# S5 outer products in a pool of their own, temporaries shared with the powers, a third read-back buffer

## The chip, the core and the metric

One core of a Trainium2 chip runs the whole program in one launch. TensorE does the matrix products and transposes, VectorE and ScalarE the elementwise work and the evacuation of PSUM, GpSimd a few powers, and SyncE issues the DMAs. The metric is the time of one execution on the device in microseconds, as the median of several runs.

## The reference

Two layers of a trunk with three branches (gated linear attention, latent attention, an S5 state space model) run over 512 latent tokens and 128 prompt tokens, with the same weights. The change touches only the S5 branch:

```
bu = einsum('blgp,gnp->blgn', u.reshape(b, n, 32, 16), b_re + i b_im)
for d in (forward, backward):
    ab, cf = discretise(a[d], log_dt[d])         # per group and state
    x = scan(x[t] = ab * x[t-1] + cf * bu[t])    # complex, over the tokens
    y += Re(einsum('blgn,gpn->blgp', x, c))
out = glu(gelu(y + d_skip * u)); new_state_s5 = last x of each direction
```

`new_state_s5` and the S5 output of both token groups are results or feed them.

## The kernel before, in words

All tokens stand side by side (640 columns). Weights are streamed through SBUF in halves of 128x512: SyncE loads a raw tile `wraw`, ScalarE casts it to `whi`, VectorE subtracts to get the residue `wlo`, and TensorE multiplies three times (high by high, high by residue, residue by high). Each of these tiles has four buffers. `h` is the normalised input, made of a cast on ScalarE and a residue on VectorE too, once per layer and 128 rows.

The S5 branch works in chunks of 8 tokens, 80 chunks in all. Its input projection is written to DRAM (`sud`) and read back with one chunk to a partition: `s5_in` does that in four blocks, each with a read-back (`s5cr`, SyncE), a cast into another order (`s5cg`, ScalarE), eight transposes (line 824, TensorE) and a copy to `U`. Ahead of it, `s5_kernel` makes the kernel within a chunk; its tiles (`s5ks` among them) are written to DRAM by four `kd` DMAs. After it, `s5_z` turns chunk inputs into chunk states in 16 steps n, one for each block b of four groups and each direction d. A step's front forms `s5r` by three VectorE operations over 128x512 (a first product, line 736; a second product into `s5rtmp`, line 737; an add, line 738), transposes it on TensorE (line 845) and copies it to `s5pm` on ScalarE. Its back, one step later, multiplies `s5pm` with `U`. `s5_pow` forms the first 16 powers of the chunk's transition by four doublings of six VectorE operations (lines 890 to 895); the scan behind `s5_z` needs them.

TensorE's order is written out by hand: `fill(n)` puts n steps of a waiting projection between the S5 steps, each step six products of 320 columns (line 247). On the other engines a scheduler sets the order from priorities and its own estimate of time. The S5 stage has a raised priority, the powers a lowered one within it (`POW`). Pools are stacked: a pool that is opened after another has closed takes its memory, and a tile in it waits for the readers and writers of the tiles that lay there. `s5i` and `s5z` thus lie in the same place one after the other, and `s5i` lies where the tiles of `s5_kernel` lay.

Of the kernel before, what the change touches and what calls it, by code (L numbers as in the profile page):

```python
# [10 lines left out]
F32 = mybir.dt.float32  # L11
# [12 lines left out]
NC8 = 80  # L24
NB = 16
# [161 lines left out]
POW = 300  # L187
# [16 lines left out]
class Prog:  # L204
# [16 lines left out]
    def pool(self, name, bufs=1, **kw):  # L221
        return self.es.enter_context(self.tc.tile_pool(name=name, bufs=bufs, **kw))
# [586 lines left out]
    def s5_in(self, pa, p, fill):  # L809

        sud = self.sud[self.l]
        U = pa.tile([128, 32, NC8], F32, name="s5u")
        for cb in range(4):
            cr = p.tile([NC8, 8, 128], F32, name="s5cr", tag="s5cr", bufs=2)
            c = slice(128 * cb, 128 * cb + 128)
            self.S.dma_start(cr, sud[:, c].rearrange("(c j) x -> c j x", j=8))
            cg = p.tile([NC8, 8, 8, 16], F32, name="s5cg", tag="s5cg", bufs=1)
            self.copy(cg, cr.rearrange("c j (g x) -> c g j x", g=8))
            fill(FILL[0] if cb == 0 else FILL[1])
            for hf in range(2):  # L820
                ps = self.bank()
                for i in range(4):
                    g = 4 * hf + i
                    self.T.transpose(ps[:, NC8 * i:NC8 * i + NC8], cg[:, g].rearrange("c j x -> c (j x)"), self.ident[0:NC8, 0:NC8])
                g0 = 8 * cb + 4 * hf
                self.copy(U[:, g0:g0 + 4, :], ps[:, 0:4 * NC8].rearrange("p (g c) -> p g c", g=4))
        self.U = U

    def s5_z(self, p, fill):
        V = self.V  # L830

        X = self.mx().rearrange("p (c g) -> p c g", g=32)
        XZ = (X[:, 0:81], X[:, 82:162])
        sh = [128, 4, 8, 16]
        def front(b, d):
            r = p.tile([128, 4, 8, 16], F32, name="s5r", tag=f"s5r{d}", bufs=2 + d)
            tmp = p.tile([128, 4, 8, 16], F32, name="s5rtmp", tag=f"s5rtmp{d}", bufs=1)
            g = slice(32 * d + 4 * b, 32 * d + 4 * b + 4)
            w = [self.w[:, :, i, g].rearrange("p e g -> p g e") for i in range(2)]
            if d == 0:  # L840
                w = [x[:, :, ::-1] for x in w]
            self.outer(V, p, r, tmp, w[0], w[1], self.B1[:, 4 * b:4 * b + 4], self.B2[:, 4 * b:4 * b + 4], sh)
            ps = self.bank()
            for i in range(4):
                self.T.transpose(ps[:, 128 * i:128 * i + 128], r[:, i].rearrange("p a b -> p (a b)"), self.ident)
            pm = p.tile([128, 512], F32, name="s5pm", tag="s5pm", bufs=3)
            self.copy(pm, ps)
            return pm

        def back(b, d, pm):  # L850
            pz = self.bank()
            for i in range(4):
                self.mm(pz[:, NC8 * i:NC8 * i + NC8], pm[:, 128 * i:128 * i + 128], self.U[:, 4 * b + i, :])
            z = pz[:, 0:4 * NC8].rearrange("p (g c) -> p c g", g=4)
            gs = slice(4 * b, 4 * b + 4)
            if d == 0:
                self.copy(XZ[0][:, 1:81, gs], z)
            else:
                self.copy(XZ[1][:, 0:79, gs], z[:, 1:80])

        todo = []
        for n in range(16):
            todo.append((n // 2, n % 2, front(n // 2, n % 2)))
            if n:
                back(*todo.pop(0))
            fill(FILL[2])
        back(*todo.pop(0))
        x0 = self.vec("x0")
        V.tensor_copy(X[:, 81, :], XZ[1][:, 63, :])
        V.tensor_copy(XZ[0][:, 0, :], x0[:, 0:32])  # L870
        V.tensor_copy(XZ[1][:, 63, :], x0[:, 32:64])
        V.memset(XZ[0][:, 64, :], 0.0)
        V.memset(XZ[1][:, 79, :], 0.0)
        self.X, self.XZ = X, XZ

    def s5_pow(self, p):

        pt = p.tile([128, 2, NB, 64], F32, name="s5pt")
        V = self.V
        for i in range(2):  # L880
            V.tensor_copy(pt[:, i, 0], self.ab[:, i])
        n = 1
        while n < NB:
            sh = [128, n, 64]
            a, b = (pt[:, i, 0:n] for i in range(2))
            c, d = (pt[:, i, n - 1][:, None, :].to_broadcast(sh) for i in range(2))
            t1 = p.tile([128, NB // 2, 64], F32, name="sp1", tag="sp1")[:, 0:n]
            t2 = p.tile([128, NB // 2, 64], F32, name="sp2", tag="sp2")[:, 0:n]
            o = [pt[:, i, n:2 * n] for i in range(2)]
            V.tensor_tensor(t1, a, c, op=ALU.mult)  # L890
            V.tensor_tensor(t2, b, d, op=ALU.mult)
            V.tensor_tensor(o[0], t1, t2, op=ALU.subtract)
            V.tensor_tensor(t1, a, d, op=ALU.mult)
            V.tensor_tensor(t2, b, c, op=ALU.mult)
            V.tensor_tensor(o[1], t1, t2, op=ALU.add)
            n *= 2
            yield
        self.pt = pt
# [588 lines left out]
    def fill(self, n):  # L1487

        for _ in range(n):
            while self.stand:  # L1490
                try:
                    next(self.stand[0])
                    break
                except StopIteration:
                    self.stand.pop(0)
# [24 lines left out]
    def layer(self, l, x):  # L1520
        tc = self.tc
        self.l = l
        self.layer_vecs()
        pool = lambda n, **kw: self.pool_(n, l, **kw)
        run = lambda g: [None for _ in g]
        step = lambda g, n: [next(g, None) for _ in range(n)]
        fill = self.fill
# [5 lines left out]
        if l == 0:  # L1533
# [8 lines left out]
            g = pair(0, 8000)  # L1542
            both(g, 2)
            n = self.h_rstd()
# [5 lines left out]
        else:  # L1550
            g = self.h_rstd()
# [9 lines left out]
        es, ek, pk, pa, pz, kern = self.s5  # L1561
# [25 lines left out]
        pk.close()  # L1587
        self.late_vecs()
        with tc.high_priority(2000):
            with pool("s5i") as p:  # L1590
                self.s5_in(pa, p, fill)
            ep = ExitStack()
            pt = ep.enter_context(pool("s5t", side="right"))
            with tc.high_priority(-POW):
                for _ in self.s5_pow(pt):
                    pass
            with pool("s5z") as p:
                self.s5_z(p, fill)
        ek.close()
        with ExitStack() as eg:  # L1600
            with es:
# [81 lines left out]
```

## Time and profile before

| | |
|---|---|
| median of 3 runs | 1574.49 us (1572.39 to 1583.06) |
| the profiled execution | 1574.24 us, span 1572.5 us |
| TensorE busy | 1506.5 us, 96% of the span |
| VectorE busy | 1054.3 us, 67% |
| ScalarE busy | 629.5 us, 40% |
| mean granted TensorE clock | 0.986 of 2.4 GHz |

TensorE is the engine that sets the time. Times in the rows are microseconds from the span's start; PE is TensorE, DVE VectorE, ACT ScalarE, SP SyncE. Layer 0 has its S5 stage at about 100 to 170, layer 1 at about 860 to 930.

### The profile page before, as it was taken

What the parts mean: (1) busy time and instruction counts of PE and PEld (TensorE: products, weight loads), DVE (VectorE), ACT (ScalarE), POOL (GpSimd) and SP (SyncE); (2) the same over time, 40 slices, a digit from 0 to 9 for tenths busy, and PEclk for the clock granted to TensorE, in tenths of its full rate; (3) what the DMA queues carried; (4) which work ended last, traced back from release to release, by engine and by line L of the source; (5) the groups of instructions that cost most, each with busy time, mean ns of one, the idle gap of its engine ahead of it and who ended that gap; (6) DMA issues with size and microseconds to landing.
All of it is one profiled execution on the core that took longest, in us unless ns stands there. A gap on an engine that the chain in (4) does not pass through costs nothing. (4 is left out here: it accounts for less than half of the span.)

```text
span 1572.5 us, 28798 instructions
## 1 busy us (share of the span) xinstructions
PE 1506.5 (96%) x11334; PEld 1436.7 (91%) x11334; DVE 1054.3 (67%) x2435; ACT 629.5 (40%) x1171; POOL 46.5 (3%) x48
## 2 busy tenths in 40 slices
PE   5998999999999999999999899999999999999998
PEld 3788999988999888898998899999999999888998
DVE  8979694796556536879577579645766563487662
ACT  3324323555444454322324442254544442633321
POOL 0000000011000000000000000001300000000000
PEclk9998999999999999999999999999999999999999
DMA  9451435243312221237753333442331223212253
GB/s 347 158 151 49 122 113 167 90 133 102 103 63 75 85 75 56 78 110 241 258 195 99 97 79 113 138 133 87 115 114 61 74 81 111 69 55 68 91 169 104
DMA packets 109656, 182.09 MB, mean 116 GB/s; under 512 B 12752, under 2 KB 31120, under 8 KB 109520
## 3 DMA queue, kind: packets, MB, share of 16 engines
q1 hardware_dynamic: 109520, 180.25, 36.3%
q8 instruction: 89, 1.46, 0.4%
q14 instruction: 47, 0.39, 0.1%
HBM read 150.41 MB, written 29.79 MB: 115 GB/s over the span
## 5 line engine op out<-in xcount | busy, mean ns | idle before, releaser
L247 PE MATMUL pj<-h,whi 128*128 128x320 f32 x3456 | 664.8, 314 | 0.2 <-DVE og L488 0.2
L247 PEld LDWEIGHTS pj<-h,whi 128*128 128x128 f32 x3456 | 541.7, 189 | 6.5 <-issue 5.1
L229 ACT ACTIVATE whi<-wraw 128x512 fp32r<-128x512 f32 x326 | 204.9, 630 | 517.3 <-PE pj L247 384.1
L247 PE MATMUL pj<-h,wlo 128*128 128x320 f32 x1728 | 397.6, 310 | 0.0
L238 DVE TENSOR_TENSOR wlo<-wraw,whi 128x512 fp32r<-128x512 f32 x326 | 223.9, 688 | 216.5 <-ACT whi L229 209.8
L247 PEld LDWEIGHTS pj<-h,wlo 128*128 128x128 f32 x1728 | 290.8, 189 | 0.0
L247 PE MATMUL pj<-og,whi 128*128 128x320 f32 x736 | 142.9, 314 | 2.4 <-DVE og L238 2.4
L247 PEld LDWEIGHTS pj<-og,whi 128*128 128x128 f32 x736 | 115.4, 189 | 6.9 <-DVE og L238 3.2
L247 PE MATMUL pj<-whi,h 128*128 128x512 f32 x256 | 86.6, 400 | 5.1 <-ACT h L232 4.4
L247 PE MATMUL pj<-og,wlo 128*128 128x320 f32 x384 | 87.8, 310 | 0.0
L247 PEld LDWEIGHTS pj<-whi,h 128*128 128x128 f32 x256 | 48.8, 192 | 17.4 <-ACT h L232 5.0
L247 PEld LDWEIGHTS pj<-og,wlo 128*128 128x128 f32 x384 | 64.5, 188 | 0.0
L232 ACT ACTIVATE P<-bank,smx 128x384 f32<-128x384 f32 x64 | 36.5, 576 | 49.8 <-DVE smx L1235 49.8
L238 DVE TENSOR_TENSOR Ptl<-bank,Pth 128x512 fp32r<-128x512 f32 x48 | 31.7, 687 | 31.1 <-ACT Pth L229 30.9
L232 ACT ACTIVATE th<-pj 128x640 f32<-128x640 f32 x72 | 49.7, 690 | 6.3 <-PE pj L247 6.2
L247 PE MATMUL pj<-wlo,h 128*128 128x512 f32 x128 | 50.6, 396 | 0.0
L247 PE MATMUL pj<-s5g,whi 128*128 128x320 f32 x256 | 48.1, 310 | 0.0
L247 PE MATMUL bank<-s5qy,mx 128*80 128x128 f32 x256 | 46.1, 302 | 0.0
L577 DVE SCALAR_TENSOR_TENSOR mx<-pj,ada,tmp 128x320 f32<-128x320 f32 (+2 forms) x48 | 18.1, 433 | 39.6 <-PE pj L247 37.5
L1231 DVE TENSOR_REDUCE smx<-bank 128x1 f32<-128x384 f32 (+1 forms) x72 | 36.5, 524 | 10.6 <-PE bank L247 10.0
L229 ACT ACTIVATE Pth<-bank 128x512 fp32r<-128x512 f32 x48 | 27.1, 596 | 35.3 <-PE bank L1256 35.3
L1421 DVE SCALAR_TENSOR_TENSOR st<-st,bl,bank 64x128 f32<-64x128 f32 x112 | 38.8, 347 | 3.5
(349 smaller groups left out, 2320.2 us busy)
## 6 DMA issues: line engine op xcount, KB each, us to landing
wraw<-wpk SPq DMA_DIRECT2D x358, 256.0 KB, 2.8
og<-wpk SPq DMA_DIRECT2D x48, 256.0 KB, 5.4
qd<-s5qk SPq DMA_DIRECT2D x32, 256.0 KB, 2.9
s5qy<-qd SPq DMA_DIRECT2D x32, 256.0 KB, 4.0
gd<-gt SPq DMA_DIRECT2D x16, 320.0 KB, 2.8
gt<-gd SPq DMA_DIRECT2D x16, 320.0 KB, 3.1
md<-th SPq DMA_DIRECT2D x16, 320.0 KB, 2.3
th<-md SPq DMA_DIRECT2D x16, 320.0 KB, 3.5
```

What stands on the lines that cost most here:

```text
L229: self.A.activation(out, in_, AF.Copy, scale=scale)
L232: self.A.activation(out, in_, f, **kw)
L238: (eng or self.V).tensor_tensor(lo, src, hi.bitcast(F32), op=ALU.subtract)
L247: self.T.matmul(out, lhsT, rhs, start=start, stop=stop, skip_group_check=True, **kw)
L577: V.scalar_tensor_tensor(xn[:, j, lo:hi], ps[:, i, lo - 320 * i:hi - 320 * i], self.ads[l, 2][r][:, j:j + 1], xr[:, lo:hi], op0=ALU.mult, ...
L1231: V.tensor_reduce(mx[:, i:i + 1], ps[:, 0:w], axis=AX.X, op=ALU.max)
L1421: V.scalar_tensor_tensor(out, st[r, c, :], bl[r, c:c + 1], pu[c][r], op0=ALU.mult, op1=ALU.add)
```

## The change

`s5r` and `s5rtmp` move from the pool `s5z` to a new pool `s5r`, which is opened ahead of `s5i`, so that it lies beside `s5i` and not in its place. The first direction keeps two buffers of `s5r`, the second has two instead of three. The powers no longer have temporaries of their own (`sp1`, `sp2`): they use the two `s5rtmp` tiles, by the tags `s5rtmp0` and `s5rtmp1`. The read-back `s5cr` has three buffers instead of two.

```diff
--- before.py
+++ after.py
@@ -811,7 +811,7 @@
         sud = self.sud[self.l]
         U = pa.tile([128, 32, NC8], F32, name="s5u")
         for cb in range(4):
-            cr = p.tile([NC8, 8, 128], F32, name="s5cr", tag="s5cr", bufs=2)
+            cr = p.tile([NC8, 8, 128], F32, name="s5cr", tag="s5cr", bufs=3)
             c = slice(128 * cb, 128 * cb + 128)
             self.S.dma_start(cr, sud[:, c].rearrange("(c j) x -> c j x", j=8))
             cg = p.tile([NC8, 8, 8, 16], F32, name="s5cg", tag="s5cg", bufs=1)
@@ -826,15 +826,15 @@
                 self.copy(U[:, g0:g0 + 4, :], ps[:, 0:4 * NC8].rearrange("p (g c) -> p g c", g=4))
         self.U = U
 
-    def s5_z(self, p, fill):
+    def s5_z(self, pr, p, fill):
         V = self.V
 
         X = self.mx().rearrange("p (c g) -> p c g", g=32)
         XZ = (X[:, 0:81], X[:, 82:162])
         sh = [128, 4, 8, 16]
         def front(b, d):
-            r = p.tile([128, 4, 8, 16], F32, name="s5r", tag=f"s5r{d}", bufs=2 + d)
-            tmp = p.tile([128, 4, 8, 16], F32, name="s5rtmp", tag=f"s5rtmp{d}", bufs=1)
+            r = pr.tile([128, 4, 8, 16], F32, name="s5r", tag=f"s5r{d}", bufs=2)
+            tmp = pr.tile([128, 4, 8, 16], F32, name="s5rtmp", tag=f"s5rtmp{d}", bufs=1)
             g = slice(32 * d + 4 * b, 32 * d + 4 * b + 4)
             w = [self.w[:, :, i, g].rearrange("p e g -> p g e") for i in range(2)]
             if d == 0:
@@ -873,7 +873,7 @@
         V.memset(XZ[1][:, 79, :], 0.0)
         self.X, self.XZ = X, XZ
 
-    def s5_pow(self, p):
+    def s5_pow(self, p, pr):
 
         pt = p.tile([128, 2, NB, 64], F32, name="s5pt")
         V = self.V
@@ -884,8 +884,8 @@
             sh = [128, n, 64]
             a, b = (pt[:, i, 0:n] for i in range(2))
             c, d = (pt[:, i, n - 1][:, None, :].to_broadcast(sh) for i in range(2))
-            t1 = p.tile([128, NB // 2, 64], F32, name="sp1", tag="sp1")[:, 0:n]
-            t2 = p.tile([128, NB // 2, 64], F32, name="sp2", tag="sp2")[:, 0:n]
+            t1 = pr.tile([128, 4, 8, 16], F32, name="s5rtmp", tag="s5rtmp0").rearrange("p a b c -> p (a b c)")[:, 0:64 * n].rearrange("p (n g) -> p n g", g=64)
+            t2 = pr.tile([128, 4, 8, 16], F32, name="s5rtmp", tag="s5rtmp1").rearrange("p a b c -> p (a b c)")[:, 0:64 * n].rearrange("p (n g) -> p n g", g=64)
             o = [pt[:, i, n:2 * n] for i in range(2)]
             V.tensor_tensor(t1, a, c, op=ALU.mult)
             V.tensor_tensor(t2, b, d, op=ALU.mult)
@@ -1587,15 +1587,16 @@
         pk.close()
         self.late_vecs()
         with tc.high_priority(2000):
-            with pool("s5i") as p:
-                self.s5_in(pa, p, fill)
             ep = ExitStack()
             pt = ep.enter_context(pool("s5t", side="right"))
-            with tc.high_priority(-POW):
-                for _ in self.s5_pow(pt):
-                    pass
-            with pool("s5z") as p:
-                self.s5_z(p, fill)
+            with pool("s5r") as pr:
+                with pool("s5i") as p:
+                    self.s5_in(pa, p, fill)
+                with tc.high_priority(-POW):
+                    for _ in self.s5_pow(pt, pr):
+                        pass
+                with pool("s5z") as p:
+                    self.s5_z(pr, p, fill)
         ek.close()
         with ExitStack() as eg:
             with es:
```

TensorE's instructions and their order are the same. On VectorE in layer 0, around the end of the powers, this stood before:

```order
L895 TENSOR_TENSOR s5pt<-sp_1502,sp_1503 128x512
L238 TENSOR_TENSOR wlo<-wraw,whi 128x512 x2
L736 TENSOR_TENSOR s5r<-s5w,s5b 128x512
L737 TENSOR_TENSOR s5rtmp<-s5w,s5b 128x512
L736 TENSOR_TENSOR s5r<-s5w,s5b 128x512
L737 TENSOR_TENSOR s5rtmp<-s5w,s5b 128x512
L736 TENSOR_TENSOR s5r<-s5w,s5b 128x512 x3
L738 TENSOR_TENSOR s5r<-s5r,s5rtmp 128x512 x2
```

and this stands now:

```order
L893 TENSOR_TENSOR s5rtmp<-s5pt 128x512
L894 TENSOR_TENSOR s5rtmp<-s5pt 128x512
L895 TENSOR_TENSOR s5pt<-s5rtmp 128x512
L737 TENSOR_TENSOR s5rtmp<-s5w,s5b 128x512 x2
L738 TENSOR_TENSOR s5r<-s5r,s5rtmp 128x512 x2
L238 TENSOR_TENSOR wlo<-wraw,whi 128x512
L737 TENSOR_TENSOR s5rtmp<-s5w,s5b 128x512 x2
L736 TENSOR_TENSOR s5r<-s5w,s5b 128x512
L738 TENSOR_TENSOR s5r<-s5r,s5rtmp 128x512
```

The first products of four steps are no longer here: they stand ahead of the powers, right before the copies into `s5pt`. The second products follow the last power, and one residue stands behind the adds that stood before the products.

On SyncE's queue in layer 0, from the last `kd` DMA on, with what each waits for (DMAHW are eight DMA semaphores taken in turn; the four `kd` DMAs have 0, 1, 2 and 4, and a DMA waits for its own semaphore's last use too), before:

```order
L792 DMA kd_98<-s5ks 128x1x240 [waits DMAHW4_49]
L816 DMA s5cr<-sud_102 80x8x128 [waits DMAHW2_49,DMAHW4_49,DMAHW1_49,DMAHW5_49,DMAHW0_49,PE_49]
L816 DMA s5cr<-sud_102 80x8x128 [waits DMAHW6_49]
L268 DMA wraw<-wpk 128x512 [waits DMAHW7_49,DVE_49]
L816 DMA s5cr<-sud_102 80x8x128 [waits DMAHW5_49,Activation_49]
L268 DMA wraw<-wpk 128x512 [waits DVE_49] x2
L268 DMA wraw<-wpk 128x512 [waits DMAHW3_49,DVE_49]
L816 DMA s5cr<-sud_102 80x8x128 [waits DMAHW6_49,Activation_49]
```

and now:

```order
L792 DMA kd_98<-s5ks 128x1x240 [waits DMAHW4_49]
L816 DMA s5cr<-sud_102 80x8x128 [waits DMAHW5_49,PE_49]
L816 DMA s5cr<-sud_102 80x8x128 [waits DMAHW6_49]
L816 DMA s5cr<-sud_102 80x8x128 [waits DMAHW7_49]
L816 DMA s5cr<-sud_102 80x8x128 [waits DMAHW5_49,DMAHW0_49,Activation_49]
L268 DMA wraw<-wpk 128x512 [waits DMAHW1_49,DVE_49]
L268 DMA wraw<-wpk 128x512 [waits DMAHW2_49,DVE_49]
```

The four read-backs stand together, and the first no longer waits for the `kd` DMAs.

On VectorE in layer 1, in the middle of the chain that makes `h` (here the `kd` DMAs have the semaphores 7, 0, 1 and 2), before:

```order
L238 TENSOR_TENSOR wlo<-wraw,whi 128x512 [waits DMAHW1_49,Activation_49]
L881 COPY s5pt<-s5ab 128x64 [waits DMAHW4_49,DMAHW6_49,DMAHW2_49,DMAHW0_49]
L881 COPY s5pt<-s5ab 128x64
L459 SCALAR_TENSOR_TENSOR h<-mx,ada_8575,h 128x512 [waits DVE_49]
L459 SCALAR_TENSOR_TENSOR h<-mx,ada_8575,h 128x128 [waits Activation_49]
L459 SCALAR_TENSOR_TENSOR mx<-mx,ada_9425,th 128x512 [waits DMAHW4_49]
L459 SCALAR_TENSOR_TENSOR mx<-mx,ada_9425,th 128x128
L890 TENSOR_TENSOR sp_10096<-s5pt 128x64 [waits DVE_49]
```

and now:

```order
L238 TENSOR_TENSOR wlo<-wraw,whi 128x512 [waits DMAHW1_49,Activation_49]
L736 TENSOR_TENSOR s5r<-s5w,s5b 128x512 [waits DMAHW2_49,DMAHW1_49,DMAHW7_49,DMAHW0_49,DVE_49]
L736 TENSOR_TENSOR s5r<-s5w,s5b 128x512 x3
L881 COPY s5pt<-s5ab 128x64 x2
L459 SCALAR_TENSOR_TENSOR h<-mx,ada_8579,h 128x512 [waits DVE_49]
L459 SCALAR_TENSOR_TENSOR h<-mx,ada_8579,h 128x128 [waits Activation_49]
L459 SCALAR_TENSOR_TENSOR mx<-mx,ada_9429,th 128x512 [waits DMAHW4_49]
L459 SCALAR_TENSOR_TENSOR mx<-mx,ada_9429,th 128x128
L238 TENSOR_TENSOR wlo<-wraw,whi 128x512 [waits DMAHW4_49,Activation_49]
```

Four first products stand ahead of the `h` residues now, and the first of them waits for the `kd` DMAs; in layer 0 the four stand in the same way ahead of the powers, with the same wait.

## Rows read from the trace of the kernel before

**Rows 1.** The page, part 1: busy time, share, instructions.
```profile
PE 1506.5 (96%) x11334; PEld 1436.7 (91%) x11334; DVE 1054.3 (67%) x2435; ACT 629.5 (40%) x1171; POOL 46.5 (3%) x48
```

**Rows 2.** TensorE's waits over the span: total, times, longest.
```profile
PE bank L845 <- DVE s5r L738: 11.4, 2, 6.1
```

**Rows 3.** VectorE in order of time, layer 0: start, duration, idle before and its releaser.
```profile
112.86 0.69 DVE L238 TENSOR_TENSOR wlo<-wraw,whi 128x512 fp32r<-128x512 f32 x1 [5.48 <-ACT whi L229]
...
114.40 0.42 DVE L890 TENSOR_TENSOR sp<-s5pt 128x256 f32<-128x256 f32 x1
...
122.46 0.68 DVE L238 TENSOR_TENSOR wlo<-wraw,whi 128x512 fp32r<-128x512 f32 x1
...
126.65 0.69 DVE L736 TENSOR_TENSOR s5r<-s5w,s5b 128x512 f32<-128x512 f32 x1
...
130.86 1.28 DVE L738 TENSOR_TENSOR s5r<-s5r,s5rtmp 128x512 f32<-128x512 f32 x2
```

**Rows 4.** TensorE in order of time, layer 0.
```profile
125.54 0.87 PE L824 MATMUL bank<-c,s5cg 80*128 80x80 f32 x8 [1.84 <-ACT s5cg L229]
131.69 1.08 PE L845 MATMUL bank<-c,s5r 128*128 128x128 f32 x4 [5.29 <-DVE s5r L738]
...
137.42 0.60 PE L845 MATMUL bank<-c,s5r 128*128 128x128 f32 x4
137.86 1.02 PE L247 MATMUL bank<-s5u,s5pm 128*128 128x80 f32 x8
138.67 0.83 PE L247 MATMUL pj<-h,whi 128*128 128x320 f32 x4
...
139.63 0.60 PE L845 MATMUL bank<-c,s5r 128*128 128x128 f32 x4
```

**Rows 5.** Stretches: length, busy time of each engine (instructions), granted clock, DMA share.
```profile
132.00:136.00 4.00, 4.00 (x19) 3.96 (x18) 4.00 (x8) 1.19 (x2) 0.00 (x0) 0.50 0.00 0
398.00:400.00 2.00, 1.07 (x9) 0.82 (x8) 0.94 (x3) 0.26 (x3) 0.00 (x0) 1.00 0.35 121
400.00:402.00 2.00, 2.00 (x18) 2.00 (x17) 1.29 (x2) 1.08 (x2) 0.00 (x0) 1.00 0.03 10
```

**Rows 6.** TensorE in order of time, layer 1.
```profile
886.23 0.77 PE L824 MATMUL bank<-c,s5cg 80*128 80x80 f32 x8 [1.18 <-ACT s5cg L229]
893.11 1.09 PE L845 MATMUL bank<-c,s5r 128*128 128x128 f32 x4 [6.11 <-DVE s5r L738]
...
898.72 0.49 PE L845 MATMUL bank<-c,s5r 128*128 128x128 f32 x3
```

**Rows 7.** SyncE's DMA issues in order of time, layer 0.
```profile
103.19 0.76 SPq L792 DMA_DIRECT2D kd<-s5ks  x1
106.71 1.28 SPq L816 DMA_DIRECT2D s5cr<-sud  x2
108.08 0.58 SPq L268 DMA_DIRECT2D wraw<-wpk  x1
112.33 0.56 SPq L816 DMA_DIRECT2D s5cr<-sud  x1
...
120.45 0.57 SPq L816 DMA_DIRECT2D s5cr<-sud  x1
```

**Rows 8.** The tile s5ks, both layers: issues (ns, first and last start), time to landing.
```profile
L792 SPq DMA_DIRECT2D kd<-s5ks x8: 581/646/937, 99.9 to 837.6; - x8
...
DMA to landing us min/median/max: 3.1/3.7/4.1
```

**Rows 9.** Groups by line and shape on VectorE, layer 0: busy us, mean ns.
```profile
L890 DVE TENSOR_TENSOR sp<-s5pt 128x128 f32<-128x128 f32 x1 | 0.3, 291 | 0.0
...
L890 DVE TENSOR_TENSOR sp<-s5pt 128x64 f32<-128x64 f32 x1 | 0.2, 226 | 0.0
```

**Rows 10.** VectorE's fourth h residue in layer 1, and TensorE's first use of it.
```profile
839.85 1.01 DVE L459 SCALAR_TENSOR_TENSOR h<-mx,ada,h 128x512 fp32r<-128x512 f32 x2
...
845.43 0.61 PE L247 MATMUL pj<-whi,h 128*128 128x512 f32 x2
```

## The prediction

> **What bounds the kernel now.** I read the page's busy shares first, then the waits of TensorE, then the order of time around its two longest S5 waits, engine by engine, and last the granted clock there. TensorE is busy for 96% of the span [rows 1], and its instructions and their order stay as they are, so the change can only take away time in which TensorE waits or runs at a lower clock. One wait belongs to the lines that the diff touches: the transposes of line 845 waited twice, 11.4 us in all, for `s5r` [rows 2], once in each layer.
>
> In layer 0 the reader is to see a chain. The powers end at 122.46, where a weight residue starts; the seven products of `s5r` and `s5rtmp` ahead of the first add start only at 126.65, after the last chunk transposes have freed the tiles in the same memory, and that add starts at 130.86 [rows 3]. TensorE waited 1.84 us for the fourth chunk's cast and then 5.29 us for the add, and started line 845 at 131.69, 0.83 us after the add's start [rows 4]. After that it ran at a granted clock of 0.50, the 1.2 GHz level [rows 5], so that the third group of transposes began at 137.42, 5.73 us after the first. At full clock a step takes 2.21 us (137.42 to 139.63), and the first has no state products behind it (0.81 us, 137.86 to 138.67), so 2 x 2.21 - 0.81 = 3.61 us would do: 2.1 us went to the clock. Layer 1 is the same: 1.18 us, then 6.11 us, and 5.61 us from the first to the third group (893.11 to 898.72), 2.0 us of it the clock [rows 6].
>
> The Trainium skill, TensorE: Matmul & The Clock Gate, section "Part 1: The HAM clock gate", says that the engine's default is the half rate and that activity releases the full one; this trace agrees, with 0.50 after the 5.29 us.
>
> **The change, part by part.**
>
> *Third read-back buffer.* The fourth read-back went out at 120.45, when a second buffer was free; now it needs only the first cast, which had freed the third one's buffer at 112.33 [rows 7]. It lands long before its cast is due, so both chunk waits go: TensorE would reach line 824 at 125.54 - 1.84 = 123.70 and at 886.23 - 1.18 = 885.05, and line 845 some 0.72 us later, at 124.4 and 885.8. On SyncE's queue the weight load of 108.08 now stands behind the fourth read-back, up to 112.33 + 0.56 = 112.9, so 4.8 us later. Four raw and four split tiles lie between a load and its use; I cost it at nothing, and at up to 4.8 us if that cover were gone.
>
> *Products ahead of the powers, layer 0.* The pool `s5r` takes the memory of the kernel tiles, so the first product now waits for the four `kd` DMAs, which read `s5ks`. The last was issued at 103.19 [rows 7], and these land 3.1 to 4.1 us after the issue [rows 8]; the first read-back, which had the same wait, went out at 106.71 [rows 7], so I take 106.7. Queued behind it on VectorE are powers and weight residues; the residue of the half that TensorE uses three halves later has room, so nothing else waits. Then come, up to the first add: four products at 0.60 us (seven in 126.65 to 130.86 [rows 3]) 2.4; two copies 0.3; six powers of 128x64 at 0.226 and six of 128x128 at 0.291 [rows 9] 3.1; three residues 1.8 and one gate product 0.8; then the same twelve larger powers, two residues and one gate product that took 114.40 to 122.46, 8.1; then the two second products 1.2. That is 17.7 us: the first add starts at 124.4, and line 845 at 125.2, 0.8 us after TensorE is there. The third group's add starts six slots of 0.60 us after the first (an add, a residue, two second products, a product stand between), as long as TensorE's own 3.61 us, so the third group begins near 128.8 if the clock holds.
>
> Here two rows stand apart: after an idle of 0.93 us around 399 the clock stayed at 1.00, after 5.29 us it was 0.50 [rows 5]. 0.8 us is next to the first, so I take full clock. Gain of layer 0: 137.42 - 128.8 = 8.6 us, with ends: 9.4 if the add is not late at all, 6.5 if the clock falls.
>
> *The shared temporaries* are what keeps the second products behind the last power: without them the first add could be ready before 124.4. They cost the 0.8 us just counted in layer 0 and nothing in layer 1, where the adds of the first four steps stand ahead of residues that VectorE did well before line 845.
>
> *Products ahead, layer 1.* Line 845 starts at 885.8 and the third group at 885.8 + 3.61 = 889.4 instead of 898.72: 9.3 us. But the four products stand in the middle of the chain that makes `h` for the su projection. The last `kd` DMA is issued at 837.6 and lands 3.1 to 4.1 us later, 3.7 in the middle [rows 8], so at 841.3; four products at 0.60 end at 843.7, two copies at 844.0, and the fourth `h` residue, which took 1.01 us from 839.85, is now done at 845.0. TensorE reads it at 845.43 [rows 10]. It fits by 0.4 us, and with the latest landing (841.7) by nothing. I take 0 as the cost and keep 0.5.
>
> The Trainium skill, Perfetto Trace Analysis, section "Tensor Engine Instruction", says that VectorE and ScalarE take their queues strictly first in, first out. That is the rule against this change: a product that waits for a DMA holds the `h` residues behind it. By it the sum loses whatever the landing is later than 841.7.
>
> *Two buffers instead of three for direction 1.* A product of step n waits for the transposes of step n - 4. Three VectorE operations of 0.60 us a step are 1.8 us against TensorE's 2.21 [rows 3, 4], so VectorE gains on TensorE and two buffers do: nothing, and 0.4 us a step at most if a residue falls badly. The powers' own six operations a doubling are unchanged in number. Further down, some `kt` and `st` operations change places on VectorE; no row prices it, and I allow 2 us either way.
>
> **The sum.** The profiled execution took 1574.24 us (span 1572.5, 1.7 around it), 0.25 under the median of 1574.49. 8.6 + 9.3 = 17.9 us less gives 1556.3 for it and 1556.6 against the median. I predict 1556.5, 1.1% faster.
>
> **Rivals.** *A, layer 0 keeps part of its wait.* If the chunk casts come no earlier than before, the second residue of the row holds VectorE until 112.86, as it did [rows 3]; the rest up to the add (0.6 + 4.1 + 8.1 + 1.2 = 14.0) ends at 126.9, line 845 starts at 127.7 after 3.3 us of idle, and the clock stays low: 4.0 us instead of 8.6, so 1561.2. Against it: the first read-back no longer waits for the landing of `kd` but follows its last issue (103.19 and 0.76 us), so it goes out some 2.7 us earlier than 106.71 [rows 7]. For it: every operation in that row must be on time.
>
> *B, the clock falls after the short wait.* Then layer 0 gains 6.5: 1558.7. The section of the clock gate page named above gives this result if 0.8 us is enough; the row at 399 says it isn't.
>
> *C, nothing gained.* The pool order does not let the products start early enough in either layer, or other waits open behind: 1570 to 1575. The order on VectorE speaks against it, since the products do stand ahead.
>
> *D, slower.* The four products of layer 1 hold the `h` chain. Each microsecond of landing beyond 841.7 is one of TensorE at the su projection, and some 2 more once for the clock. It decides from a landing near 858, 20 us after the issue, where landings took 3.1 to 4.1 us; at 23 us it gives 1577.
>
> **How the numbers follow.** Forecast 0.58 (1554.5 to 1558.5), A 0.19, B 0.10, C 0.09, D 0.04. The range 1554 to 1564 takes in A and B and leaves out C, D and a little of the forecast's own ends. Within 1% is what a measurement here can't tell from no change; the line is at 1558.7. B is split by it. Faster 0.61, same 0.35, slower 0.04.
>
> **What would show it.** In the changed profile: no wait at line 824; at line 845 under 1.5 us in layer 0 and none in layer 1; granted clock 1.00 from 120 to 140 and from 880 to 900; the fourth read-back issued right after the first cast; TensorE without a gap near 845. A wait of 3 us at line 845 in layer 0 is A, a clock of 0.50 after a short one B, a TensorE gap at the fourth su step D. What would make the forecast wrong is a landing of `kd` far later than 4 us, now that the read-backs go out beside it, or an `h` chain with less room than the 0.4 us.

## Result, and the profile after

The changed kernel takes 1557.55 us (median of 6 runs, 1555.72 to 1562.57) against 1574.82 of before (6 runs): a ratio of 0.9888, 95% interval 0.9862 to 0.9915. That is 17.3 us less; 1556.5 was predicted. Twice more, beside other kernels, its median was 1556.17 and 1555.62, where the kernel before had 1575.19 and 1575.93: 19.0 and 20.3 us less.

The profiled execution has a span of 1554.9 us, 17.6 less than before. First the page's busy row, then TensorE's waits by releaser (total, times, longest), to be held against [rows 1, 2]:

```profile
PE 1501.9 (97%) x11334; PEld 1433.3 (92%) x11334; DVE 1054.4 (68%) x2435; ACT 629.1 (40%) x1171; POOL 46.7 (3%) x48
```

```profile
PE bank L247 <- ACT kt L229: 2.5, 1, 2.5
PE bank L845 <- DVE s5r L738: 2.1, 1, 2.1
```

The wait for `s5r` is 2.1 us, once, where it was 11.4 in two; the wait for the cast at line 824 is no longer listed. TensorE did the same 11334 matrix products and transposes. In order of time, layer 0 and then layer 1 (start, duration, idle before and its releaser; before: [rows 4, 6]):

```profile
116.70 0.72 PE L824 MATMUL bank<-c,s5cg 80*128 80x80 f32 x8
...
123.76 0.72 PE L824 MATMUL bank<-c,s5cg 80*128 80x80 f32 x8
126.56 0.63 PE L845 MATMUL bank<-c,s5r 128*128 128x128 f32 x4 [2.08 <-DVE s5r L738]
127.91 0.60 PE L845 MATMUL bank<-c,s5r 128*128 128x128 f32 x4
130.17 0.63 PE L845 MATMUL bank<-c,s5r 128*128 128x128 f32 x4
...
870.32 0.72 PE L824 MATMUL bank<-c,s5cg 80*128 80x80 f32 x8
...
877.39 0.72 PE L824 MATMUL bank<-c,s5cg 80*128 80x80 f32 x8
877.95 0.60 PE L845 MATMUL bank<-c,s5r 128*128 128x128 f32 x4
879.27 0.60 PE L845 MATMUL bank<-c,s5r 128*128 128x128 f32 x4
881.60 0.60 PE L845 MATMUL bank<-c,s5r 128*128 128x128 f32 x4
```

Neither layer waits for a cast. Layer 0 waits 2.08 us for the add, layer 1 not at all. From the first to the third group of line 845 it is 3.61 and 3.65 us, where it was 5.73 and 5.61. The stretches with the granted clock (the third number from the right; 1.00 is full speed) stand for [rows 5]:

```profile
126.00:128.00 2.00, 1.44 (x11) 1.47 (x12) 2.00 (x4) 0.60 (x1) 0.00 (x0) 1.00 0.00 0
128.00:130.00 2.00, 2.00 (x19) 2.00 (x17) 2.00 (x5) 1.03 (x2) 0.00 (x0) 1.00 0.41 131
```

Behind the wait of 2.08 us the clock stays at 1.00. What ended that wait is read from ScalarE, VectorE and SyncE, each in order of time (before: [rows 3, 7]):

```profile
110.30 1.06 ACT L229 ACTIVATE s5cg<-s5cr 80x1024 f32<-80x1024 f32 x1 [5.38 <-DMA s5cr<-sud]
111.26 0.61 ACT L229 ACTIVATE whi<-wraw 128x512 fp32r<-128x512 f32 x1
```

```profile
107.48 2.50 DVE L736 TENSOR_TENSOR s5r<-s5w,s5b 128x512 f32<-128x512 f32 x4 [4.63 <-DMA kd<-s5ks]
...
111.91 0.69 DVE L238 TENSOR_TENSOR wlo<-wraw,whi 128x512 fp32r<-128x512 f32 x1 [0.85 <-ACT whi L229]
...
124.52 1.29 DVE L737 TENSOR_TENSOR s5rtmp<-s5w,s5b 128x512 f32<-128x512 f32 x2
125.73 1.28 DVE L738 TENSOR_TENSOR s5r<-s5r,s5rtmp 128x512 f32<-128x512 f32 x2
```

```profile
103.88 0.77 SPq L792 DMA_DIRECT2D kd<-s5ks  x1
104.74 7.19 SPq L816 DMA_DIRECT2D s5cr<-sud  x4
```

The four products waited for `kd`, as forecast. But VectorE then waits again, 0.85 us, for a `whi`, and that stood on ScalarE behind the first read-back's cast, which waited for the read-back's landing. From the residue at 111.91 to the add at 125.73 VectorE has no gap to speak of, so in this profile the chain that sets the add is the read-back's, not that of `kd`. The two chains end close together, though. In changed_third the same residue starts without a listed wait, and the add follows the products by 17.51 us instead of 18.25; the wait at line 845 is 1.60 us all the same:

```profile
109.31 2.50 DVE L736 TENSOR_TENSOR s5r<-s5w,s5b 128x512 f32<-128x512 f32 x4 [4.90 <-DMA kd<-s5ks]
...
113.00 0.69 DVE L238 TENSOR_TENSOR wlo<-wraw,whi 128x512 fp32r<-128x512 f32 x1
...
126.82 1.28 DVE L738 TENSOR_TENSOR s5r<-s5r,s5rtmp 128x512 f32<-128x512 f32 x2
```

For what follows, the way through the program is cut at rows of TensorE: the start of the first line 824 and of the third group of line 845 in each layer, and the end of the span. Each entry is a difference of two such rows of one profile; in kernels with code added line 845 has another number.

```
kernel                          to L824  L0 stage  between  L1 stage    rest    span
before                           116.47     20.95   740.39     20.91  673.78  1572.5
changed                          116.70     13.47   740.15     11.28  673.30  1554.9
changed_again                    115.97     13.05   739.77     11.27  672.64  1552.7
changed_third                    118.26     13.00   737.14     11.26  672.84  1552.5
e1_third_buffer_only             117.16     19.52   742.63     19.44  672.95  1571.7
e2_two_readback_buffers          115.59     12.78   739.24     12.33  674.66  1554.6
e3_own_temporaries               116.17     12.16   744.67     12.44  674.86  1560.3
e6_pool_other_side               116.56     15.90   737.34     11.28  672.72  1553.8
e4_first_steps_ahead_both        116.43     11.27   742.25     11.28  675.07  1556.3
e5_first_steps_ahead_layer0      116.05     11.28   742.47     11.28  674.52  1555.6
e8_layer0_ahead_again            116.61     11.28   742.42     11.28  674.51  1556.1
e7_delay_before_first_add        116.80     19.73   740.23     11.29  671.25  1559.3
```

The gain lies in the two stages: 7.5 to 8.0 us in layer 0 and 9.6 in layer 1 in the three profiles of the changed kernel, 17.1 to 17.6 together. The long stretch between scatters by up to 3 us between profiles of one kernel, so small effects are read from the stages. Much of that scatter is the granted clock. An estimate from the clock of the stretch between, its length times the share not granted, gives 6.8, 6.8 and 5.1 us for the three profiles of the changed kernel, and the third is also the one that is 2.6 to 3.0 us shorter there; it gives 6.8 for the kernel before and, with the kernels named by the start of their labels, 5.1 for e6, 6.8 for e2, 8.5 for e4, and 10.2 for e1, e3, e5, e7 and e8.

### The profile page after: what moved, and what is told of

Its sections match the earlier page's. It is cut to its first block, busy times and chain, and to the rows that moved or that the text cites. A ratio compares the mean times of both kernels' runs of the same rounds, so it can differ in the third digit from the quotient of the medians.

```text
span 1554.9 us, 28794 instructions
## 1 busy us (share of the span) xinstructions
PE 1501.9 (97%) x11334; PEld 1433.3 (92%) x11334; DVE 1054.4 (68%) x2435; ACT 629.1 (40%) x1171; POOL 46.7 (3%) x48
## 5 line engine op out<-in xcount | busy, mean ns | idle before, releaser
L247 PEld LDWEIGHTS pj<-whi,h 128*128 128x128 f32 x256 | 48.7, 191 | 17.7 <-ACT h L232 5.3
```

Source lines behind the costliest of these rows:

```text
L247: self.T.matmul(out, lhsT, rhs, start=start, stop=stop, skip_group_check=True, **kw)
```

## Experiments

**The third read-back buffer by itself**, on the kernel before:

```diff
-            cr = p.tile([NC8, 8, 128], F32, name="s5cr", tag="s5cr", bufs=2)
+            cr = p.tile([NC8, 8, 128], F32, name="s5cr", tag="s5cr", bufs=3)
```

> The kernel before with the third read-back buffer and nothing else. My theory: the products of the first step wait for the last chunk transposes, so both chunk waits (1.84 and 1.18 us) go and everything behind moves up by as much, while the waits of 5.3 and 6.1 us at line 845 and the granted clock of 0.50 behind them stay: about 3.0 us less than before, a span near 1569.5. Rival 1: the wait is only moved, line 845 waits 7.1 and 7.3 us and the span stays at 1572.5. Rival 2: the buffer is the larger part of the whole gain, span under 1563.

Measured: 1571.33 us (10 runs) against 1574.50 (13), a ratio of 0.9978 (0.9964 to 0.9992), so 3.2 us less. TensorE in layer 0 and layer 1:

```profile
124.23 0.72 PE L824 MATMUL bank<-c,s5cg 80*128 80x80 f32 x8
130.46 1.09 PE L845 MATMUL bank<-c,s5r 128*128 128x128 f32 x4 [5.50 <-DVE s5r L738]
...
893.34 1.09 PE L845 MATMUL bank<-c,s5r 128*128 128x128 f32 x4 [6.23 <-DVE s5r L738]
```

The chunk waits are gone, the waits at line 845 stay almost as long (5.50 and 6.23 instead of 5.29 and 6.11), and each stage is 1.4 to 1.5 us shorter, 2.9 in all. The theory holds, both rivals fall. The profile's own span shows only 0.8, because the stretch between is 2.2 us longer (the granted clock was 0.70 and 0.50 from 824 to 832 there, where the kernel before had 1.00); the medians' 3.2 agrees with the 2.9 (its interval is 1.3 to 5.7 us).

**Two read-back buffers in the changed kernel**, the same line the other way.

> The changed kernel with two read-back buffers, as before. My theory: in layer 0 the wait at line 824 comes back (1.8 us), but the add of the first step is ready when it was (line 845 near 126.6), so its wait there shrinks from 2.1 to about 0.3 us and layer 0 loses 0 to 0.3; in layer 1, where line 845 has no wait, 1.2 us are lost: 1.2 to 1.5 us more than the changed kernel, a span near 1556.3. Rival: the parts add up, 3.0 us more, a span near 1558.

Measured: 1558.28 us (4 runs), ratio 0.9885 (0.9869 to 0.9901), the same as the changed kernel's. Where the buffer is missing:

```profile
122.87 0.77 PE L824 MATMUL bank<-c,s5cg 80*128 80x80 f32 x8
124.75 0.63 PE L845 MATMUL bank<-c,s5r 128*128 128x128 f32 x4 [1.11 <-DVE s5r L738]
...
875.79 0.77 PE L824 MATMUL bank<-c,s5cg 80*128 80x80 f32 x8 [0.94 <-ACT s5cg L229]
```

The stage of layer 1 is 1.06 us longer (12.33 against 11.27), that of layer 0 no longer at all (12.78 against 13.00 to 13.47). The chunk wait of layer 0, which I expected back at 1.8 us, is 0.2 (122.87 is 2.56 us behind the third block's start at 120.31, the others 2.36), since the fourth read-back went out at 117.80 and not at 120.45 as in [rows 7]; there the expectation was wrong. Its sum, 1.2 to 1.5 us, was too high as well: the two stages together are 0.4 to 0.8 us longer. What holds is that the parts don't add up, against the rival's 3.0: by stages the buffer is worth 2.9 us alone, and 0.4 to 0.8 beside the other edits.

**Temporaries of their own for the powers** (with two read-back buffers, since three don't fit beside them):

```diff
-            t1 = pr.tile([128, 4, 8, 16], F32, name="s5rtmp", tag="s5rtmp0")...
-            t2 = pr.tile([128, 4, 8, 16], F32, name="s5rtmp", tag="s5rtmp1")...
+            t1 = p.tile([128, NB // 2, 64], F32, name="sp1", tag="sp1")[:, 0:n]
+            t2 = p.tile([128, NB // 2, 64], F32, name="sp2", tag="sp2")[:, 0:n]
```

> The changed kernel with temporaries of their own for the powers; as both don't fit, two read-back buffers. To be held against the run with two read-back buffers and shared temporaries. By the order on VectorE six products and two adds of the first steps now stand ahead of the powers. My theory: layer 0 has no wait at line 845 any more, 0 to 0.3 us less than with shared ones, since line 824 waits 1.8 us there in any case; in layer 1 two more products, 1.2 us, stand ahead of the fourth h residue and then two adds and two products ahead of the next ones, so TensorE waits in the su projection, 1.2 to 3 us in all: 1 to 3 us slower than with two buffers and shared temporaries, span 1557 to 1559.5. Rival: the h chain has room, own temporaries are the better choice, the span is at or under that of the run with two buffers.

Measured: 1561.18 us (4 runs, 1557.40 to 1562.04), 2.9 over the run with shared ones (1556.36 to 1558.56); with four runs each and ranges that overlap this isn't clear of the scatter. The span is 5.7 longer. Layer 0 has no wait for the add any more (12.16 against 12.78; line 824 waits 0.77 us there, not the 1.8 expected), and in layer 1 TensorE waits twice in the su projection:

```profile
838.60 0.73 PE L247 MATMUL pj<-whi,h 128*128 128x512 f32 x2 [0.27 <-DVE h L459]
843.10 0.72 PE L247 MATMUL pj<-whi,h 128*128 128x512 f32 x2 [0.80 <-DVE h L459]
```

The direction is the theory's: 1.07 us of waits there, against none in the changed kernel. The stretch between is 5.4 us longer; the granted clock was 0.62 and 0.52 from 816 to 824 as well, ahead of these waits, so not all of the 5.4 is theirs: by the estimate above 3.4 us more are lost to the clock (10.2 against 6.8).

**The pool at the other end of the memory**: products and temporaries no longer stand where the `kd` DMAs read.

```diff
-            with pool("s5r") as pr:
+            with pool("s5r", side="right") as pr:
```

> The changed kernel with the pool of the products and temporaries at the other end of the memory, where the DMAs that store the kernel pieces (line 792) don't read; the order on VectorE, ScalarE and TensorE is the same. My theory: the 4.63 us and 2.19 us that VectorE waited for those DMAs at line 736 go, the four products of layer 0 start near 102.9 instead of 107.5, the powers end earlier and line 845 waits 0 to 0.5 us instead of 2.1; layer 1 gains nothing on TensorE, since it doesn't wait there: about 1.6 to 2.1 us less than the changed kernel, a span near 1553. Rival: VectorE then waits for a weight residue that comes no earlier (one stands between the products and the powers, and waits for ScalarE behind the read-back's cast), and the add is no earlier: no change, 1554.9.

Measured: 1559.30 us (4 runs), ratio 0.9893 (0.9871 to 0.9915). ScalarE, VectorE and TensorE in layer 0:

```profile
111.04 1.06 ACT L229 ACTIVATE s5cg<-s5cr 80x1024 f32<-80x1024 f32 x1 [6.27 <-DMA s5cr<-sud]
```

```profile
102.63 2.49 DVE L736 TENSOR_TENSOR s5r<-s5w,s5b 128x512 f32<-128x512 f32 x4
...
112.66 0.69 DVE L238 TENSOR_TENSOR wlo<-wraw,whi 128x512 fp32r<-128x512 f32 x1 [6.46 <-ACT whi L229]
...
126.47 1.28 DVE L738 TENSOR_TENSOR s5r<-s5r,s5rtmp 128x512 f32<-128x512 f32 x2
```

```profile
127.30 0.63 PE L845 MATMUL bank<-c,s5r 128*128 128x128 f32 x4 [2.95 <-DVE s5r L738]
128.87 1.05 PE L845 MATMUL bank<-c,s5r 128*128 128x128 f32 x4
132.46 0.60 PE L845 MATMUL bank<-c,s5r 128*128 128x128 f32 x4
```

The rival's mechanism holds, and my theory falls; that nothing would change did not come true, since the stage is 2.4 us longer (15.90 against 13.47). The products start 4.85 us earlier than in the changed kernel, and the add 0.74 later. The block input's pool now lies where `kd` is read, so the read-backs went out at 107.14 instead of 104.74, and the cast came at 111.04. From the cast's start to the add it is 15.43 us here (111.04 to 126.47), 15.43 in the changed kernel (110.30 to 125.73), and 15.43 with two read-back buffers (108.49 to 123.92). So the add comes no earlier than that behind the cast, however early the products start. Behind the wait of 2.95 us the granted clock was 0.59 and 0.56 in the next two stretches of 2 us, and it is 5.16 us to the third group.

**The first four steps' adds ahead of the powers**, with shared temporaries and three buffers: the body of `front` that makes `r` becomes a method, called for n = 0 to 3 ahead of the powers.

```diff
+                ready = [self.s5_r(pr, n // 2, n % 2) for n in range(4)]
                 with tc.high_priority(-POW):
                     for _ in self.s5_pow(pt, pr):
                         pass
                 with pool("s5z") as p:
-                    self.s5_z(pr, p, fill)
+                    self.s5_z(pr, p, fill, ready)
...
-            self.outer(V, p, r, tmp, w[0], w[1], ...)
+            r = ready.pop(0) if ready else self.s5_r(pr, b, d)
```

> The changed kernel with the first four steps' products and adds written ahead of the powers, in both layers; shared temporaries and three read-back buffers stay. Theory after the first four runs: in layer 0 the adds no longer stand behind the weight residue that waits for the read-back's cast, nor behind the powers, so the wait of 2.1 us at line 845 goes; in layer 1 two more products (1.2 us) stand ahead of the fourth h residue, then adds and products ahead of the next ones, so TensorE waits 0.8 us or more in the su projection and the clock falls behind it, some 2.5 us, as with own temporaries: 0 to 1.5 us more than the changed kernel. Rival: the loss of layer 1 with own temporaries came from their order or from the two read-back buffers, the h chain has room, and this kernel is 2 us faster than the changed one.

Measured: 1556.98 us (4 runs), ratio 0.9883 (0.9868 to 0.9897); the changed kernel beside it 1556.17. Both halves of the theory show, and the 0.8 us more lie within its 0 to 1.5, though not by the way that it names. Layer 0's stage is 11.27 us, the length without any wait, and in layer 1 the su projection waits:

```profile
835.96 0.74 PE L247 MATMUL pj<-whi,h 128*128 128x512 f32 x2 [0.17 <-DVE h L459]
840.32 0.73 PE L247 MATMUL pj<-whi,h 128*128 128x512 f32 x2 [0.67 <-DVE h L459]
```

The clock stayed at 1.00 around them, so the 2.5 us for a fall of the clock there were wrong; the waits make 0.84. The stretch between is 2.1 us longer than the longest of the changed kernel all the same. By the estimate above 1.7 us more are lost to the clock there, at another place: from 604 to 608 the granted clock was 0.57, where that changed profile has 1.00, and in both TensorE had waited 2.40 us just there, at line 247 for `fin` (604.71 and 607.33).

**The same in layer 0 alone** (`range(0 if l else 4)`), run twice:

> The same, in layer 0 alone; layer 1 as in the changed kernel. Theory: no wait at line 845 in layer 0, the third group of transposes 2.1 us earlier against line 824, 9.7 us less than before between the first line 824 and the third group (7.6 in the changed kernel); layer 1 as there: 2.1 us less than the changed kernel, the best of all versions, near 1555.5 as a median. Rival: the powers, 2.4 us later on VectorE, hold what comes behind them, the scan or a later step's add, and the gain is given back.

> The kernel with layer 0's first four steps ahead of the powers, again: its profile had the 2.2 us of layer 0, but lower granted clock near 816 and 1048 that the changed kernel didn't have there, and its median was no lower. Theory 1: those falls of the clock come and go with where the execution happens to stand, and with more runs the median is 1 to 2.5 us under the changed kernel's in the same call. Theory 2: they belong to this kernel's order or timing, the profile shows both again, and the median is within 1 us of the changed kernel's.

> The changed kernel once more, beside the others on the same chip, as the base for differences of 1 to 3 us: 1556 to 1559 as a median; line 845 in layer 0 waits 1 to 3 us, set by the landing of the first read-back.

> The changed kernel beside it. Theory 1: a median 1 to 2.5 us above the other's. Theory 2: within 1 us of it, and no fall of the clock near 816 and 1048 in its profile.

Measured: 1557.80 and 1558.20 us (4 and 6 runs) against 1556.17 and 1555.62 (4 and 5 runs) of the changed kernel beside it, so the 1555.5 that was expected of this kernel was missed by 2.3. The changed kernel's own expectation came true, with waits of 1.65 and 1.60 us at line 845. The stage gains what was forecast: 11.28 us, 1.7 to 2.2 less, with no wait at the transposes (here line 849):

```profile
123.12 0.72 PE L824 MATMUL bank<-c,s5cg 80*128 80x80 f32 x8
123.67 0.60 PE L849 MATMUL bank<-c,s5r 128*128 128x128 f32 x4
```

In these two profiles it is given back far from there. The stretch between takes 742.4 us instead of 737.1 to 740.2, and the rest 674.5 instead of 672.6 to 673.3. Stretches of the first and of the second run of this kernel, and then of changed_third, near the two places:

```profile
816.00:820.00 4.00, 3.33 (x30) 2.41 (x27) 0.43 (x4) 0.28 (x1) 0.00 (x0) 0.51 0.43 143
1046.00:1050.00 4.00, 4.00 (x27) 4.00 (x27) 2.80 (x6) 1.76 (x3) 2.74 (x2) 0.78 0.20 68
```

```profile
816.00:820.00 4.00, 3.24 (x34) 1.90 (x31) 0.43 (x4) 0.28 (x1) 0.41 (x1) 0.56 0.51 175
1046.00:1050.00 4.00, 4.00 (x30) 4.00 (x29) 2.43 (x5) 1.93 (x3) 2.22 (x2) 0.82 0.21 72
```

```profile
816.00:820.00 4.00, 3.03 (x45) 1.94 (x46) 0.60 (x5) 0.28 (x1) 1.16 (x1) 1.00 0.82 287
1046.00:1050.00 4.00, 4.00 (x30) 4.00 (x30) 2.24 (x4) 0.74 (x1) 2.69 (x2) 1.00 0.19 66
```

Both profiles of this kernel have the falls of the clock, none of the three of the changed kernel has: that is theory 2's sign. Its median is not: 1.6 and 2.6 us over the changed kernel's, where theory 2 said within 1 and theory 1 said 1 to 2.5 under. The ranges are nearly the same (1554.33 to 1560.62 in ten runs, 1554.32 to 1559.93 in nine), so neither a gain nor a loss is clear of the scatter. That the falls belong to this kernel is not shown by two profiles: in the changed kernel itself the clock fell at 604 to 608 in one profile (0.65) and not in the other two (1.00). What stands is that a kernel with a better stage shows no gain as a whole, and no other kernel run here does over the changed one. Of the rival's later add nothing is seen: TensorE has no wait at the transposes of any later step.

**A longer wait by added work**: in layer 0, in the last doubling of the powers, one product of 128x512 is formed five times more, into the same tile, so that the values stay as they are.

```diff
             V.tensor_tensor(t1, a, d, op=ALU.mult)
+            if self.l == 0 and n == NB // 2:
+                for _ in range(5):
+                    V.tensor_tensor(t1, a, d, op=ALU.mult)
```

> The changed kernel with five more VectorE products of 128x512 (0.60 us each, results not used) in layer 0 ahead of the first add, so that the wait of 2.1 us at line 845 becomes 5.1. Theory: the granted clock behind it falls to 0.50 as in the kernel before, the way from the first to the third group of transposes takes 5.6 to 5.8 us instead of 3.6, and 5.1 us are lost against the changed kernel. Rival: the clock stays at 1.00 and only the 3.0 us of the products are lost; then the 2.1 us that I put down to the clock came from VectorE's rate in the first steps.

Measured: 1557.81 us (4 runs, 1555.90 to 1561.05), ratio 0.9891 (0.9874 to 0.9909). In layer 0:

```profile
130.14 1.09 PE L845 MATMUL bank<-c,s5r 128*128 128x128 f32 x4 [5.55 <-DVE s5r L738]
...
136.53 0.60 PE L845 MATMUL bank<-c,s5r 128*128 128x128 f32 x4
```

```profile
132.00:136.00 4.00, 4.00 (x20) 3.96 (x19) 4.00 (x8) 1.03 (x2) 0.00 (x0) 0.50 0.00 0
```

The clock falls, and first to third group takes 6.39 us: the stage is 6.3 us longer than in the changed kernel, 3.5 of it wait and 2.8 clock. The rival, 3.0 alone, falls. The profile's span is 4.4 us longer than the changed kernel's (1559.3 against 1554.9), the median only 1.6; the profiled execution was the slowest of the four. Two places where some of it comes back are seen. The added products also changed ScalarE's order behind the stage, and TensorE's wait of 2.5 us for `kt`, listed above for the changed kernel, is not in this kernel's waits. And the last part of the table, the rest, is 1.4 to 2.1 us shorter.

## Why the prediction was right, step by step

**The sum.** 17.9 us were forecast, 8.6 and 9.3. The stages gave 7.5 to 8.0 and 9.6. A surplus of 0.3 in layer 1 makes up for part of the shortfall in layer 0, and the time came out within 1.1 us. That it is so near is in part luck: the other two medians lie 19.0 and 20.3 us under the kernel before, and a stretch that the forecast takes as unchanged varies by 3 us between profiles.

**The third read-back buffer** took away both chunk waits, as said. It was not priced on its own; alone it is worth 2.9 us by stages and 3.2 by medians, within the whole under 1.

**Products ahead, layer 0: the term that was mis-sized.** The forecast let the first add start at 124.4 and line 845 wait 0.8 us. The add started at 125.73, and the wait was 2.08, 1.65 and 1.60 us in three profiles, each over the 1.5 us that the prediction named as its own sign. Two steps share the 1.3 us. "I take 106.7": the products started at 107.48, 0.8 later, behind a last `kd` issue at 103.88 instead of 103.19. "So nothing else waits": the row waited once more, 0.85 us, for a `whi` behind the read-back's cast. The row's own length was right: 17.7 us were forecast, and it is 17.51 in changed_third, where no wait is listed in it. There the late start alone leaves a wait of 1.60 us.

Rival A had the right chain for the first profile: it took 14.0 us from the second residue to the add, and it was 13.8 (111.91 to 125.73). Its price was too high, since the residue came at 111.91 and not at 112.86, and since the clock did not fall. The read-back went out right behind the last `kd` issue (104.74 behind 103.88), but took 5.6 us to its cast, where it had taken 4.5 before (106.71 to 111.24).

The Trainium skill, Perfetto Trace Analysis, section "Tensor Engine Instruction (MATMUL, LD_WEIGHTS)", says that ScalarE and VectorE work their queues strictly first in, first out. The equal 15.43 us from cast to add agree with it: a `whi` that needs no read-back stood behind the cast that does, on one engine, and the powers behind its residue, on the other.

**The clock.** "If the clock holds": it held at a wait of 2.08 us, and 3.61 us to the third group is the very figure of the sum. It did not hold at 2.95 and 5.55 us. The price of its fall was put at 2.1; the run with the added products shows 2.8, the one with the pool at the other end 1.55 (5.16 against 3.61). Rival B didn't come true in any of the three profiles. But the reason given, that the wait is near the 0.93 us of the row at 399, doesn't reach to 2.08, so this is luck as far as the runs show: elsewhere in the same profile the clock was 0.57 from 524 to 528, behind a wait of 1.88 us (524.69), and behind two waits of one length it held once and fell once. The same twenty products take 1.31 us at the first of these and 1.97 at the second:

```profile
607.33 1.31 PE L247 MATMUL bank<-c,la 128*64 128x128 f32 x20 [2.40 <-DVE fin L1421]
...
657.15 1.97 PE L247 MATMUL bank<-c,la 128*64 128x128 f32 x20 [2.41 <-DVE fin L1421]
```

**The shared temporaries** were to cost 0.8 us in layer 0 and nothing in layer 1. In layer 0 it is the whole remaining wait: with the adds ahead of the powers the stage is 1.7 to 2.2 us shorter. What the prediction didn't see is their use in layer 1: by keeping the second products behind the powers they also keep two products and two adds out of the `h` chain. With own temporaries, or with the adds written ahead, TensorE waits 0.8 to 1.1 us there.

**Products ahead, layer 1.** "It fits by 0.4 us": four products cost no wait. With own temporaries, and with the adds ahead, one first product ran ahead of the landing of `kd` and five stood behind it, so that the fourth residue came 0.5 us later, counted from the end of the wait for `kd` (3.13 and 3.12 us against 2.62), and TensorE waited 0.27 and 0.17 us for it; the longer waits, 0.80 and 0.67, came at the next residue, behind two adds. So the room was real, some 0.2 to 0.3 us by these rows. Rival D needed a landing 20 us after the issue; VectorE's wait for `kd` there was 2.19 us.

**Two buffers for direction 1** cost nothing on TensorE: from the third group of line 845 to the sixteenth it takes 28.77 to 28.80 us in both layers of all twelve profiles, the kernel before, with three buffers, included.

## What to carry to other kernels

Follow every wait of the row that you move ahead, not only the first one: on an engine that works its queue in order, the wait that ends last sets the end, and it can come from a third engine that serves both chains. When time is saved before the end of a long program, look in the profile at what comes behind: here the 2 us that one edit gained in a stage were lost again, in both its profiles, at places 700 and 900 us later, and why there is open. Where profiles of one kernel differ by as much, compare the stage and say of the whole only what many runs show. And parts of a change are priced together: the buffer that is worth 2.9 us alone is worth under 1 beside the other edits.

## What was not expected of the hardware

The granted clock fell at 1046 to 1050 in a stretch where TensorE's row shows no idle time. Ahead of it stand twenty products of one column. TensorE in the second run of the kernel with layer 0 ahead, and then in the changed kernel:

```profile
1046.33 2.29 PE L247 MATMUL bank<-c,gt 128*128 128x1 f32 x20
1048.48 1.35 PE L247 MATMUL pj<-s5g,whi 128*128 128x320 f32 x4
```

```profile
1046.33 2.29 PE L247 MATMUL bank<-c,gt 128*128 128x1 f32 x20
1048.48 0.83 PE L247 MATMUL pj<-s5g,whi 128*128 128x320 f32 x4
```

The same twenty stand in every kernel here; the fall came in both runs of this one and with two read-back buffers, with own temporaries and with the adds ahead in both layers, and in no other profile. The two profiles shown have the twenty at the same time from the span's start, and still the clock is 0.64 from 1048 to 1050 in the first and 1.00 in the second, so these products and their time alone don't decide it. Nor does the length of a wait alone, by the rows on the clock above. What does wasn't tried, and stays open.
